# Probabilities times values in the window attention: whole fp32 in two column halves, in place of three fp32r passes

## Chip, cores and metric

One core of a Trainium2 chip runs the whole program. The metric is the device time of one execution in microseconds (us), as the median of several.

## What is computed

Two layers of a decoder trunk over 1024 tokens with 16 learned meta tokens ahead of them. The change lies in the second layer's attention: 16 query heads, 4 key/value heads, head size 64, a window of 128 in blocks of 128 queries, the meta tokens always visible, and one learned sink per head:

```python
def swa_mixer(h, wq, wk, wv, q_norm_w, k_norm_w, sinks, wo):
    q = rms_norm((h @ wq).reshape(b, l, kv, grp, d), q_norm_w) * (d ** -0.5)
    k = rms_norm((h @ wk).reshape(b, l, kv, d), k_norm_w)
    v = (h @ wv).reshape(b, l, kv, d)
    ...
    s_meta = jnp.einsum('bnikgd,bjkd->bnkgij', qb, km)
    s_band = jnp.einsum('bnikgd,bnjkd->bnkgij', qb, kband)      # this block's keys and the block's before
    valid = (rel >= 0) & (rel < SWA_WINDOW) & (n * SWA_BLOCK - SWA_BLOCK + j >= 0)
    s_band = jnp.where(valid[None, :, None, None], s_band, -jnp.inf)
    p = sink_softmax(jnp.concatenate([s_meta, s_band], -1), sink[None, None, :, :, None, None])
    orr = (jnp.einsum('bnkgim,bmkd->bnikgd', p[..., :N_META], vm)
           + jnp.einsum('bnkgij,bnjkd->bnikgd', p[..., N_META:], vband))
    return jnp.concatenate([om, orr], 1) @ wo
```

All inputs and outputs are float32.

## The kernel before

The program is: the first layer's mixer, its FFN, the attention (`swa`), and the second layer's FFN. Activations are kept transposed, features on the 128 partitions and tokens along the free dimension.

Matmuls against weights are done in three passes. An operand is split into a high part, rounded to fp32r, and a low part, the rest, also fp32r (`load_w`, `split`); `gemm` (L147) then adds high x high, high x low and low x high in PSUM. A matmul whose operands are plain F32 is done in whole fp32: the scores (`scp`, L1082), the sums of squares for the head norms (`qkp`, L981), the transposes and the meta part of the output (L1151). The trace shows each of these as two passes.

The attention works on two groups G of eight query heads. A group has two key/value heads s, one on partitions 0 to 63 and the other on 64 to 127, and four tiles t with one query head of each. `attend(G, hook)` goes through the eight query blocks n, and one pair (G, n) is called a block here, sixteen in all:

- `scores(G, n, pmq)`: per t two score matmuls, one per head s, each on its own 64 rows of the array, into two PSUM banks; ACT copies 144 columns out (L1088), VectorE puts the second half in under a mask (L1089), so that one 128-column window holds old keys above the diagonal and new keys below. Then the softmax: maximum and its follow-ups on VectorE (L1094 to L1097), exponentials on ACT (L1100), sum and reciprocal on VectorE (L1101, L1102), scaling on GpSimd (L1103), meta columns copied to `pmq` (L1104).
- `turn(pr)`: transposes a head's four probability tiles into one PSUM bank `ptp` and makes two operands: `all`, the whole 128 x 512, and `own`, the part under the mask U that belongs to this block's keys. Each has a high and a low part: ACT casts the high part (L1113), VectorE subtracts (L1114), and the mask is applied to the high part by VectorE and to the low part by GpSimd (both L1116).
- `out_block(G, n, pmq, pts)`: the weights are values. With v the values of this block and v' those of the block before, the output is v' x all + (v - v') x own. `vparts` splits v and d = v - v' into parts, ACT the high (L1124), GpSimd the low (L1125), each written into a zeroed 192-column tile `vx` whose middle 64 columns stay zero; a slice of 128 columns of it has the values of one head and zeros for the other. So both heads' passes fill all 128 output rows of the bank `po` and add up there. `mm3` makes the three passes (line L1028 in the profile); four matmuls with `vm` add the meta part (L1151), and VectorE copies `po` out (L1153). With n = 0 there is only the `own` term.

Between these pieces a planner puts work that does not depend on them: during `attend(0, ...)` the projections and head norms of group 1, during `attend(1, ...)` the output projections (`outputs`, L147 with `wo`). The planner runs a model of the engines when the program is built, and the queue of every engine is fixed by it.

PSUM in this stage has two banks for `mm`, two for the ring `a` (`ptp`, `pmp`, `po` and others take turns in it), and two pairs of banks for scores.

Of the kernel before, what the change touches and what calls it, by code (L numbers as in the profile page):

```python
# [7 lines left out]
F32 = mybir.dt.float32  # L8
F32R = mybir.dt.float32r
# [3 lines left out]
ALU = mybir.AluOpType  # L13
# [3 lines left out]
P = 128  # L17
# [65 lines left out]
def trunk(tc, hT0, w_in, w_ab, w_out, w_q, w_k, w_v, w_o, w_up, w_down, vec, cst, out):  # L83
    nc = tc.nc
    pe, ve, ac, gp, sp = nc.tensor, nc.vector, nc.scalar, nc.gpsimd, nc.sync
    ctx = ExitStack()
    with ctx:
# [29 lines left out]
        def col(i):  # L117
            return vt[:, i:i + 1]
# [7 lines left out]
        def aux(name, tag="b"):  # L126
            return banks["in"].tile([P, 512], F32, tag=tag, name=name, bufs=banks[tag])
# [817 lines left out]
        def swa(h, sqp):  # L945
# [5 lines left out]
            with tc.tile_pool(name="l1", bufs=1, reuse_waits="tile") as lp:  # L951
# [4 lines left out]
                ve.tensor_scalar(qn, col(V_QN), -0.125 / 128, None, ALU.mult)  # L956
                kn = lp.tile([P, 1], F32, name="kn")
                ve.tensor_scalar(kn, col(V_KN), -1.0 / 128, None, ALU.mult)
                zero = lp.tile([P, 1], F32, name="zero")
                ve.memset(zero, 0.0)  # L960
                qg = [[None] * 4, [None] * 4]
                kx = [None, None]
                vraw = [None, None]
                vm = [None, None]
                vx = []
                for i in range(4):
                    a = lp.tile([P, 192], F32R, name=f"vxh{i}")
                    b = lp.tile([P, 192], F32R, name=f"vxl{i}")
                    ve.tensor_copy(a, zero.broadcast_to([P, 192]))
                    ve.tensor_copy(b, zero.broadcast_to([P, 192]))  # L970
                    vx.append((a, b))

                def head_norms(d, wcol, ring=None, cs=CH):

                    for c0, n in cs:
                        x = d[:, c0:c0 + n]
                        sq = sqp.tile([P, 348], F32, tag="sq", name="sq", bufs=2)[:, :n]
                        y, z = (lp.tile([P, 348], F32, tag=nm, name=nm, bufs=2)[:, :n] for nm in ("hy", "hz"))
                        ac.activation(sq, x, AF.Square)
                        p2 = aux("qkp", ring) if ring else mmp("qkp")  # L980
                        pe.matmul(p2[:, :n], ct[:, C_BD:C_BD + P], sq, start=True, stop=True)  # L981
                        with tc.issue_after(lnexp):
                            ac.activation(y, p2[:, :n], AF.Ln, scale=1.0 / 64, bias=epsc)
                        ac.activation(y, y, AF.Exp, scale=-0.5)
                        ac.activation(z, y, AF.Square)

                        ve.scalar_tensor_tensor(z, p2[:, :n], 64 * EPS, z, ALU.add, ALU.mult)
                        ve.scalar_tensor_tensor(y, z, -192.0, y, ALU.add, ALU.mult)
                        ve.scalar_tensor_tensor(x, x, wcol, y, ALU.mult, ALU.mult)
# [16 lines left out]
                def values(G, vr):  # L1006
# [14 lines left out]
                    vm[G] = lp.tile([P, 4, P], F32, name=f"vm{G}")  # L1021
                    for t in range(4):
                        ve.tensor_scalar(vm[G][:, t, :], v4, ct[:, C_T4 + t:C_T4 + t + 1], None, ALU.mult)

                def mm3(ps, w, x, start, stop):
                    (wh, wl), (xh, xl) = w, x
                    for j, (a, b) in enumerate(((wh, xh), (wh, xl), (wl, xh))):
                        pe.matmul(ps, a, b, start=(start and j == 0), stop=(stop and j == 2))  # L1028

                def meta_queries(G):  # L1030
                    sc = lp.tile([NM, 8, NM], F32, tag="msc", name="msc")
# [31 lines left out]
                U = ct[:, C_U:C_U + P]  # L1063
# [43 lines left out]
                def turn(pr):  # L1107

                    tp = aux("ptp", "a")
                    for t in range(4):  # L1110
                        pe.transpose(tp[:, t * P:(t + 1) * P], pr[:, t, :], ident)
                    x, y = (lp.tile([P, 2, 512], F32R, tag="hl", name=nm, bufs=4) for nm in ("all", "own"))
                    ac.copy(x[:, 0, :], tp)  # L1113
                    ve.tensor_tensor(x[:, 1, :], tp, x[:, 0, :].bitcast(F32), ALU.subtract)  # L1114
                    for j, eng in enumerate((ve, gp)):
                        eng.tensor_tensor(y[:, j].rearrange("p (t i) -> p t i", t=4),  # L1116
                                          x[:, j].bitcast(F32).rearrange("p (t i) -> p t i", t=4),
                                          U.unsqueeze(1).broadcast_to([P, 4, P]), ALU.mult)
                    return x, y

                def vparts(pair, src):
                    d3 = lambda a: a.rearrange("p (a i) -> p a i", a=3)[:, 0::2, :]
                    src = src.rearrange("p (a i) -> p a i", a=2)
                    ac.copy(d3(pair[0]), src)  # L1124
                    gp.tensor_tensor(d3(pair[1]), src, d3(pair[0].bitcast(F32)), ALU.subtract)  # L1125

                def out_block(G, n, pmq, pts):

                    tok = slice(NM + n * P, NM + (n + 1) * P)
                    tp = aux("pmp", "a")  # L1130
                    pe.transpose(tp[:, :P], pmq.rearrange("p t s m -> p (t s m)"), ident)
                    pmt = lp.tile([P, P], F32, tag="pmt", name="pmt", bufs=2)
                    ac.copy(pmt, tp[:, :P])
                    v = vraw[G][:, n, :]
                    if n < 7:
                        vparts(vx[n % 2], v)
                    if n:
                        d = lp.tile([P, P], F32, tag="vd", name="vd", bufs=2)
                        gp.tensor_tensor(d, v, vraw[G][:, n - 1, :], ALU.subtract)
                        vparts(vx[2 + n % 2], d)  # L1140
                        use = [(0, vx[(n - 1) % 2]), (1, vx[2 + n % 2])]
                    else:
                        use = [(1, vx[0])]
                    po = aux("po", "a")
                    for s in range(2):
                        vs = slice(64 * s, 64 * s + P)
                        for j, w in use:
                            x = pts[s][j]
                            mm3(po, [a[:, vs] for a in w], (x[:, 0], x[:, 1]), s == 0 and j == use[0][0], s == 1 and j == 1)
                        for t in range(4 if s == 0 else 0):  # L1150
                            pe.matmul(po[:, t * P:(t + 1) * P], vm[G][:, t, :], pmt, start=False, stop=False)  # L1151
                    for t in range(4):
                        ve.tensor_copy(qg[G][t][:, tok], po[:, t * P:(t + 1) * P])  # L1153

                def attend(G, hook):
                    def first(n):
                        pmq = lp.tile([P, 4, 2, NM], F32, tag="pmq", name="pmq", bufs=2)
                        return pmq, scores(G, n, pmq)

                    nxt = first(0)  # L1160
                    for n in range(8):
                        pmq, prs = nxt
                        if n < 7:
                            nxt = first(n + 1)
                        out_block(G, n, pmq, [turn(pr) for pr in prs])
                        if n == 0:
                            meta_queries(G)
                        hook(n)
# [75 lines left out]
        with ExitStack() as st:  # L1244

            psum(st, "ps1", 2, 2, 0)
            h = swa(h, st.enter_context(tc.tile_pool(name="sqp", bufs=1, reuse_waits="tile")))
# [71 lines left out]
```

## Time and profile before

| | |
|---|---|
| time, median of 3 runs | 2404.53 us (2403.84 to 2405.23) |
| the profiled execution | 2401.72 us, span 2399.9 us |
| mean granted TensorE clock | 0.994 |
| busy: PE, DVE, ACT, POOL | 2336.4, 1655.3, 982.3, 477.0 us |
| first and last score matmul begin | 1370.5 and 1630.3 us |
| first and last pass of probabilities x values begin | 1395.6 and 1657.8 us |

PE is TensorE's matmuls, PEld its weight loads, DVE is VectorE, ACT ScalarE, POOL GpSimd. Times within the span are counted from its start. The profile names instructions by their line, with "out<-in" by the tiles' names. The duration of a single matmul in it holds its way through the array too, and the next one starts before it ends; the rate of a stream is read from the chain of waits, which gives a group's length from start to start.

### The profile page before, as it was taken

What the parts mean: (1) busy time and instruction counts of PE and PEld (TensorE: products, weight loads), DVE (VectorE), ACT (ScalarE), POOL (GpSimd) and SP (SyncE); (2) the same over time, 40 slices, a digit from 0 to 9 for tenths busy, and PEclk for the clock granted to TensorE, in tenths of its full rate; (3) what the DMA queues carried; (4) which work ended last, traced back from release to release, by engine and by line L of the source; (5) the groups of instructions that cost most, each with busy time, mean ns of one, the idle gap of its engine ahead of it and who ended that gap; (6) DMA issues with size and microseconds to landing.
All of it is one profiled execution on the core that took longest, in us unless ns stands there. A gap on an engine that the chain in (4) does not pass through costs nothing.

```text
span 2399.9 us, 40060 instructions
## 1 busy us (share of the span) xinstructions
PE 2336.4 (97%) x16060; PEld 2205.4 (92%) x16060; DVE 1655.3 (69%) x2840; ACT 982.3 (41%) x1980; POOL 477.0 (20%) x417
## 2 busy tenths in 40 slices
PE   8999999999999999999999999999799999999999
PEld 7999999999999999999999987878799999988887
DVE  8886735667877777776536578778977777778432
ACT  6545213434444444432225456656644444433110
POOL 1123323430000000022225245454000000002221
PEclk9999999999999999999999999999999999999999
DMA  4234434141222222253213100202222222235222
GB/s 138 84 122 138 160 118 142 54 174 74 80 72 80 80 80 80 74 195 118 86 61 107 45 27 19 88 27 76 103 90 81 78 79 79 80 142 166 82 66 101
DMA packets 93481, 224.83 MB, mean 94 GB/s; under 512 B 18672, under 2 KB 30264, under 8 KB 93296
## 3 DMA queue, kind: packets, MB, share of 16 engines
q1 hardware_dynamic: 93296, 222.28, 27.3%
q8 instruction: 126, 2.06, 0.4%
q14 instruction: 59, 0.48, 0.1%
HBM read 166.08 MB, written 56.15 MB: 93 GB/s over the span
## 4 chain that ended last, share of the span: by engine, by line
PE 82%; DVE 11%; ACT 3%; DMA 2%; issue 1%; POOL 0%; SPq 0%; ACTq 0%; DVEq 0%; POOLq 0%
PE mm L147 38%; PE A L825 20%; PE C L825 15%; PE po L1028 1%; DVE qt L251 1%; PE scp L1082 1%; ACT sc L1100 1%; DVE yl L171 1%; PE qkp L981 1%; DVE Xd L499 0%; DVE X L752 0%; DVE fq L497 0%; ACT xh L182 0%; PE po L1151 0%; DVE all L1114 0%
## 5 line engine op out<-in xcount | busy, mean ns | idle before, releaser
L825 PE MATMUL A<-X,whi 128*128 128x260 f32 (+1 forms) x2816 | 511.7, 283 | 6.6 <-ACT whi L814 2.5
L147 PE MATMUL mm<-y,wdh 128*128 128x346 f32 (+2 forms) x1760 | 471.1, 350 | 1.6 <-DVE r L903 1.6
L825 PEld LDWEIGHTS A<-X,whi 128*128 128x128 f32 x2816 | 432.6, 189 | 8.0 <-ACT whi L814 2.7
L825 PE MATMUL C<-X,whi 128*128 128x260 f32 (+1 forms) x2112 | 393.2, 284 | 8.1 <-DVE v L894 5.9
L825 PE MATMUL A<-X,wlo 128*128 128x260 f32 (+1 forms) x1408 | 391.9, 282 | 0.6 <-DVE wlo L815 0.6
L135 POOL TENSOR_TENSOR wdl<-wdr,wdh 128x512 fp32r<-128x512 f32 (+1 forms) x80 | 120.1, 1502 | 1310.0 <-ACT wdh L134 1305.5
L147 PEld LDWEIGHTS mm<-y,wdh 128*128 128x128 f32 x1760 | 315.1, 188 | 32.7 <-DVE r L903 2.0
L825 PEld LDWEIGHTS C<-X,whi 128*128 128x128 f32 x2112 | 330.4, 190 | 9.3 <-DVE v L894 6.3
L147 PE MATMUL mm<-y,wdl 128*128 128x346 f32 (+2 forms) x880 | 307.7, 350 | 0.0
L825 PE MATMUL C<-X,wlo 128*128 128x260 f32 (+1 forms) x1056 | 297.3, 284 | 0.0
L825 PEld LDWEIGHTS A<-X,wlo 128*128 128x128 f32 x1408 | 263.4, 189 | 0.8 <-DVE wlo L815 0.8
L939 DVE TENSOR_TENSOR h<-mm,h 128x346 f32<-128x346 f32 (+2 forms) x200 | 115.5, 584 | 201.8 <-PE mm L147 201.2
L825 PEld LDWEIGHTS C<-X,wlo 128*128 128x128 f32 x1056 | 200.2, 190 | 0.0
L147 PEld LDWEIGHTS mm<-y,wdl 128*128 128x128 f32 x880 | 165.5, 188 | 16.1 <-POOL wdl L135 0.7
L815 DVE TENSOR_TENSOR wlo<-sa,whi 128x1024 fp32r<-128x1024 f32 x44 | 53.9, 1225 | 161.4 <-ACT whi L814 161.4
L134 ACT CAST wdh<-wdr 128x512 fp32r<-128x512 f32 (+1 forms) x80 | 53.1, 663 | 254.8 <-PE mm L147 215.3
L814 ACT CAST whi<-sb 128x512 fp32r<-128x512 f32 x88 | 54.6, 621 | 133.7 <-PE C L825 131.1
L147 PE MATMUL mm<-xl,wqkvh 128*128 128x346 f32 (+1 forms) x288 | 95.3, 331 | 1.5 <-DVE xl L183 1.5
L147 PE MATMUL mm<-xh,wqkvh 128*128 128x346 f32 (+1 forms) x288 | 95.7, 335 | 0.7 <-DVE row L269 0.7
L814 ACT CAST whi<-sa 128x1024 fp32r<-128x1024 f32 x44 | 46.1, 1048 | 115.2 <-PE A L825 115.1
L147 PE MATMUL mm<-xh,wqkvl 128*128 128x346 f32 (+1 forms) x288 | 92.4, 322 | 0.0
L928 ACT CAST y<-yf 128x346 fp32r<-128x346 f32 (+2 forms) x110 | 54.6, 536 | 91.8 <-DVE yf L927 70.9
(402 smaller groups left out, 5235.3 us busy)
## 6 DMA issues: line engine op xcount, KB each, us to landing
wg<-in_w_up SPq DMA_DIRECT2D x44, 512.0 KB, 3.3
wv<-in_w_up SPq DMA_DIRECT2D x44, 512.0 KB, 3.5
wdr<-in_w_down SPq DMA_DIRECT2D x48, 256.0 KB, 2.6
fy<-sg SPq DMA_DIRECT2D x22, 520.0 KB, 2.7
yf<-fy SPq DMA_DIRECT2D x22, 520.0 KB, 4.5
fy<-sg SPq DMA_DIRECT2D x22, 516.0 KB, 2.7
yf<-fy SPq DMA_DIRECT2D x22, 516.0 KB, 3.8
wdr<-in_w_down SPq DMA_DIRECT2D x32, 320.0 KB, 3.4
```

The costliest lines, as they stand in the source:

```text
L134: ac.copy(hi, raw)
L135: eng.tensor_tensor(lo, raw, hi.bitcast(F32), ALU.subtract)
L147: pe.matmul(ps[:, :n], a[:, j, :], b[:, c0:c0 + n], start=(i == 0), stop=(i == last))
L171: ve.tensor_tensor(dst_l, src, dst_h.bitcast(F32), ALU.subtract)
L251: ve.scalar_tensor_tensor(d, buf[:, pad + c0 - i:pad + c0 - i + n], taps[W - 1 - i], tmp[:, :n], ALU.mult, ALU.add)
L814: ac.copy(hi, src)
L815: ve.tensor_tensor(lo, src, hi.bitcast(F32), ALU.subtract)
L825: pe.matmul(ps[:, b, :q], a[:, at + k, :], x[:, c], start=(start and n == 0), stop=(n == 11), skip_group_check=not start)
L928: ac.copy(yh[:, s], yf[:, s])
L939: ve.tensor_tensor(hn[m][:, s], ps[:, :n], hn[m][:, s], ALU.add)
L981: pe.matmul(p2[:, :n], ct[:, C_BD:C_BD + P], sq, start=True, stop=True)
L1028: pe.matmul(ps, a, b, start=(start and j == 0), stop=(stop and j == 2))
```

## The change

`turn` no longer splits. ACT copies the transposed probabilities to `all` in F32, VectorE multiplies the same PSUM bank with U into `own` in F32. GpSimd's mask is gone. `vparts`, `mm3`, the four `vx` pairs and their eight zeroing casts are gone; the values are used as they stand in `vraw`, and d stays on GpSimd. In `out_block` each head's matmul takes 64 columns of values as weights and writes 64 output rows: head 0 into rows 0 to 63 of `po` and head 1 into rows 64 to 127, so the two stand in different column halves of the array. There are four such matmuls in a block (two with n = 0), in whole fp32. The meta matmuls come after them instead of between the heads. The ring `hl` has eight buffers of half the size.

```diff
-                vx = []
-                for i in range(4):
-                    a = lp.tile([P, 192], F32R, name=f"vxh{i}")
-                    b = lp.tile([P, 192], F32R, name=f"vxl{i}")
-                    ve.tensor_copy(a, zero.broadcast_to([P, 192]))
-                    ve.tensor_copy(b, zero.broadcast_to([P, 192]))
...
-                    x, y = (lp.tile([P, 2, 512], F32R, tag="hl", name=nm, bufs=4) for nm in ("all", "own"))
-                    ac.copy(x[:, 0, :], tp)
-                    ve.tensor_tensor(x[:, 1, :], tp, x[:, 0, :].bitcast(F32), ALU.subtract)
-                    for j, eng in enumerate((ve, gp)):
-                        eng.tensor_tensor(y[:, j]..., x[:, j]..., U..., ALU.mult)
+                    x, y = (lp.tile([P, 512], F32, tag="hl", name=nm, bufs=8) for nm in ("all", "own"))
+                    four = lambda a: a.rearrange("p (t i) -> p t i", t=4)
+                    ac.copy(x, tp)
+                    ve.tensor_tensor(four(y), four(tp), U.unsqueeze(1).broadcast_to([P, 4, P]), ALU.mult)
...
-                    if n < 7:
-                        vparts(vx[n % 2], v)
                     if n:
                         d = lp.tile([P, P], F32, tag="vd", name="vd", bufs=2)
                         gp.tensor_tensor(d, v, vraw[G][:, n - 1, :], ALU.subtract)
-                        vparts(vx[2 + n % 2], d)
-                        use = [(0, vx[(n - 1) % 2]), (1, vx[2 + n % 2])]
+                        use = [(0, vraw[G][:, n - 1, :]), (1, d)]
...
-                    for s in range(2):
-                        vs = slice(64 * s, 64 * s + P)
-                        for j, w in use:
-                            x = pts[s][j]
-                            mm3(po, [a[:, vs] for a in w], (x[:, 0], x[:, 1]), s == 0 and j == use[0][0], s == 1 and j == 1)
-                        for t in range(4 if s == 0 else 0):
-                            pe.matmul(po[:, t * P:(t + 1) * P], vm[G][:, t, :], pmt, start=False, stop=False)
+                    for j, w in use:
+                        for s in range(2):
+                            vs = slice(64 * s, 64 * s + 64)
+                            pe.matmul(po[vs, :], w[:, vs], pts[s][j], start=(j == use[0][0]), stop=False,
+                                      skip_group_check=True)
+                    for t in range(4):
+                        pe.matmul(po[:, t * P:(t + 1) * P], vm[G][:, t, :], pmt, start=False, stop=True,
+                                  skip_group_check=True)
```

How the queues change is shown at three places. In the rows, `vxh` and `vxl` are high and low parts of values (one number for v', another for d), `vraw` the values, `vd` is d. A row of a matmul stands for one instruction of the program, "x2" for two alike; the last numbers are partitions x free size of the result. Line numbers before and after differ.

TensorE's queue at block n = 1 of group 0, before:

```order
L1028 MATMUL po<-all,vxh_13622 128x512 x2
L1028 MATMUL po<-all,vxl_13623 128x512
L1028 MATMUL po<-own,vxh_13634 128x512 x2
L1028 MATMUL po<-own,vxl_13635 128x512
L1151 MATMUL po<-pmt,vm_14354 128x128 x4
```

and after, the same block and the one behind it:

```order
L1122 MATMUL po<-all,vraw_14317 64x512 x2
L1122 MATMUL po<-own,vd 64x512 x2
L1125 MATMUL po<-pmt,vm_14336 128x128 x4
L971 MATMUL qkp<-sq,ct 128x346
L1096 MATMUL ptp<-ct,sc 128x128 x4
```

The four rows ahead of L1151 stood a second time behind it for the other head; two rows of two whole-fp32 matmuls have taken the place of all eight. In the next block the two heads of the `own` pair are parted: one L1122 row with `vd` stands alone, then come two scores, a transpose, twelve projection matmuls, and then the other.

VectorE's queue in group 1, in the blocks that have no output projections between them, before:

```order
L1094 TENSOR_REDUCE sc<-sc 128x4
L1114 TENSOR_TENSOR all<-ptp,all 128x512
L1116 TENSOR_TENSOR own<-all,ct 128x512
L1089 COPY_PREDICATED sc<-ct,scp 128x128
L1095 TENSOR_TENSOR sc<-sc,vt 128x4
```

and after:

```order
L1079 TENSOR_REDUCE sc<-sc 128x4
L1100 TENSOR_TENSOR own<-ptp,ct 128x512
L1074 COPY_PREDICATED sc<-ct,scp 128x128
L1080 TENSOR_TENSOR sc<-sc,vt 128x4
L1074 COPY_PREDICATED sc<-ct,scp 128x128
```

The subtraction has left the queue, and the mask reads PSUM.

GpSimd's queue in the same blocks, before:

```order
L1116 TENSOR_TENSOR own<-all,ct 128x512 x2
L1103 TENSOR_TENSOR sc<-sc 128x576
L1104 COPY pmq<-sc 128x4x16
L1125 TENSOR_TENSOR vxl_13627<-vraw_14959,vxh_13626 128x2x64
L1103 TENSOR_TENSOR sc<-sc 128x576
L1125 TENSOR_TENSOR vxl_13631<-vd,vxh_13630 128x2x64
L1104 COPY pmq<-sc 128x4x16
```

and after:

```order
L1088 TENSOR_TENSOR sc<-sc 128x576
L1089 COPY pmq<-sc 128x4x16
L1088 TENSOR_TENSOR sc<-sc 128x576
L1089 COPY pmq<-sc 128x4x16
L1114 TENSOR_TENSOR vd<-vraw_14915 128x128
```

The masks and the low parts of the values have left it; scaling, the meta columns and the difference stay.

More of the change, by code (lines that the diff above doesn't have):

```diff
@@ L958, in swa @@
                 ve.tensor_scalar(kn, col(V_KN), -1.0 / 128, None, ALU.mult)
-                zero = lp.tile([P, 1], F32, name="zero")
-                ve.memset(zero, 0.0)
                 qg = [[None] * 4, [None] * 4]
@@ L964, in swa @@
                 vm = [None, None]
-                vx = []
-                for i in range(4):
-                    a = lp.tile([P, 192], F32R, name=f"vxh{i}")
-                    b = lp.tile([P, 192], F32R, name=f"vxl{i}")
-                    ve.tensor_copy(a, zero.broadcast_to([P, 192]))
-                    ve.tensor_copy(b, zero.broadcast_to([P, 192]))
-                    vx.append((a, b))
                 def head_norms(d, wcol, ring=None, cs=CH):
@@ L1023, in values @@
                         ve.tensor_scalar(vm[G][:, t, :], v4, ct[:, C_T4 + t:C_T4 + t + 1], None, ALU.mult)
[L1025 to L1028, printed above, removed]
                 def meta_queries(G):
@@ L1111, in turn @@
                         pe.transpose(tp[:, t * P:(t + 1) * P], pr[:, t, :], ident)
-                    x, y = (lp.tile([P, 2, 512], F32R, tag="hl", name=nm, bufs=4) for nm in ("all", "own"))
-                    ac.copy(x[:, 0, :], tp)
-                    ve.tensor_tensor(x[:, 1, :], tp, x[:, 0, :].bitcast(F32), ALU.subtract)
-                    for j, eng in enumerate((ve, gp)):
-                        eng.tensor_tensor(y[:, j].rearrange("p (t i) -> p t i", t=4),
-                                          x[:, j].bitcast(F32).rearrange("p (t i) -> p t i", t=4),
-                                          U.unsqueeze(1).broadcast_to([P, 4, P]), ALU.mult)
-                    return x, y
[L1121 to L1125, printed above, removed]
+                    x, y = (lp.tile([P, 512], F32, tag="hl", name=nm, bufs=8) for nm in ("all", "own"))
+                    four = lambda a: a.rearrange("p (t i) -> p t i", t=4)
+                    ac.copy(x, tp)
+                    ve.tensor_tensor(four(y), four(tp), U.unsqueeze(1).broadcast_to([P, 4, P]), ALU.mult)
+                    return x, y
                 def out_block(G, n, pmq, pts):
@@ L1139, in out_block @@
                         gp.tensor_tensor(d, v, vraw[G][:, n - 1, :], ALU.subtract)
-                        vparts(vx[2 + n % 2], d)
-                        use = [(0, vx[(n - 1) % 2]), (1, vx[2 + n % 2])]
+                        use = [(0, vraw[G][:, n - 1, :]), (1, d)]
                     else:
-                        use = [(1, vx[0])]
+                        use = [(1, v)]
                     po = aux("po", "a")
-                    for s in range(2):
-                        vs = slice(64 * s, 64 * s + P)
-                        for j, w in use:
-                            x = pts[s][j]
-                            mm3(po, [a[:, vs] for a in w], (x[:, 0], x[:, 1]), s == 0 and j == use[0][0], s == 1 and j == 1)
-                        for t in range(4 if s == 0 else 0):
-                            pe.matmul(po[:, t * P:(t + 1) * P], vm[G][:, t, :], pmt, start=False, stop=False)
+                    for j, w in use:
[6 more added lines that the diff above has]
+                                  skip_group_check=True)
                     for t in range(4):
```

## The prediction

> **What bounds the kernel now.** I read the engines' shares first, then the stretches of the stage that the change touches, then the chain of waits inside them. By the shares TensorE is the bound:
>
> ```profile
> span 2399.9 us, 40060 instructions
> PE 2336.4 (97%) x16060; PEld 2205.4 (92%) x16060; DVE 1655.3 (69%) x2840; ACT 982.3 (41%) x1980; POOL 477.0 (20%) x417
> ```
>
> A share of the whole program says nothing of one stage, so I cut the attention (from 1370 to 1660 us) where its chain of waits changes engine. Columns: length, then busy time and count of PE, its weight loads, DVE, ACT and POOL, then the granted clock.
>
> ```profile
> 1370.00:1426.00 56.00, 56.00 (x365) 48.60 (x364) 39.27 (x115) 30.35 (x114) 28.31 (x32) 1.00 0.09 31
> 1426.00:1494.00 68.00, 64.08 (x367) 48.78 (x366) 55.85 (x147) 44.81 (x162) 38.97 (x45) 1.00 0.07 23
> 1494.00:1594.00 100.00, 98.11 (x593) 83.60 (x591) 73.33 (x212) 53.06 (x193) 43.84 (x51) 0.98 0.18 64
> 1594.00:1637.00 43.00, 35.46 (x199) 25.69 (x198) 36.60 (x104) 27.22 (x110) 26.93 (x31) 0.96 0.04 13
> 1637.00:1660.00 23.00, 23.00 (x143) 21.84 (x144) 16.43 (x39) 11.57 (x32) 13.12 (x10) 1.00 0.18 59
> ```
>
> PE is full, or nearly so, in the first, third and last stretch: there a microsecond of PE work is a microsecond of time. In the second it idles 3.9 us and in the fourth 7.5 us, while VectorE is busy for 82% and 85%. The chain of waits in the fourth (start, length, what) shows who holds PE up:
>
> ```profile
> 1611.78 0.60 DVE all L1114
> 1612.38 0.60 DVE own L1116
> ...
> 1613.19 0.95 DVE sc L1095
> ...
> 1614.35 0.59 DVE all L1114
> 1614.94 0.60 DVE own L1116
> 1615.54 0.66 DVE sc L1094
> 1616.20 0.51 DVE sc L1096
> ...
> 1616.74 0.51 ACT sc L1100 x2
> ...
> 1617.34 1.19 ACT sc L1100 x6
> ```
>
> So there are two prices: PE work counts in the full stretches, VectorE's chain in the other two.
>
> **PE work, before.** A block is one step n of attend for one group; there are sixteen. The chain at a block in a full stretch, and the counts of po's passes with their durations in ns (least, median, most):
>
> ```profile
> 1421.29 1.12 PE scp L1082 x8
> 1422.41 1.56 PE po L1028 x6
> 1423.97 0.89 PE po L1151 x8
> 1424.86 1.39 PE po L1028 x6
> 1426.24 0.59 PE qkp L981 x2
> ```
>
> ```profile
> L1151 PE MATMUL po<-pmt,vm x128: 270/275/402, 1396.3 to 1656.5; 128*128 128x128 f32 x128
> L1028 PE MATMUL po<-own,vxh x64: 387/396/967, 1395.6 to 1657.5; 128*128 128x512 f32 x64
> L1028 PEld LDWEIGHTS po<-own,vxh x64: 186/188/333, 1395.5 to 1657.3; 128*128 128x128 f32 x64
> ```
>
> Six passes take 1.39 us, 0.232 us each (the 1.56 includes leaving the score matmuls). A block has twelve, 2.78 us; a block with n = 0 has only the "own" half, six, 1.39 us. The four matmuls with vm are whole fp32 and stand as eight passes: a whole-fp32 matmul is two passes.
>
> **PE work, after.** A block has four whole-fp32 matmuls with 64 columns of weights and 512 moving columns, so eight passes. The price of such a pass comes from two other whole-fp32 lines:
>
> ```profile
> L621 PE MATMUL onp<-fq,ct x16: 590/592/697, 378.5 to 461.0; 128*128 128x512 f32 x16
> L981 PE MATMUL qkp<-sq,ct x60: 442/453/762, 1304.8 to 1528.1; 128*128 128x346 f32 x40, 128*128 128x334 f32 x16, 128*128 128x348 f32 x4
> ```
>
> Their medians differ by 139 ns over 166 columns: 0.84 ns per column, 0.43 us for 512 (the two qkp passes above, 346 columns, take 0.59 us, 0.85 per column). So a pass is 1.85 times as dear as before, and the change pays on PE only if the two heads run at the same time. The trace has no two matmuls in different column halves. It has its nearest kin in L1082, where the heads stand in different row halves: eight passes of 272 columns at 0.84 would be 1.83 us one after the other, and the row says 1.12: four times 0.228 = 0.91, plus 0.21 for getting into and out of the split array. Row halves thus run fully side by side. I take the same for column halves: four slots of 0.43 plus 0.21 = 1.93 us, against 2.78. The other end is eight slots, 3.65 us. With n = 0 it is 1.07 or 1.93 us, against 1.39. Fourteen blocks save 0.85 and two save 0.32: 12.5 us; in one block the order puts twelve projection matmuls between the two heads' "own" matmuls, which costs two lone passes, 0.86. PE: **-11.7 us** side by side, and one after the other 14 x 0.87 + 2 x 0.54 = **+13.3 us**. I take the first, by the row of L1082.
>
> The Trainium skill's page "TensorE: Matmul & The Clock Gate" (Part 3) says that column tiles run concurrently much as row tiles do and gives 2.38 times for three of them; by it the PE term is the first one, and no run so far shows it for whole fp32. The same section says that a weight load overlaps a running matmul only if their row groups differ, which two column halves never do; that is the last rival below.
>
> **VectorE and GpSimd.** The change takes out the subtraction L1114, GpSimd's half of L1116 and both lines of vparts, and leaves L1116 on VectorE, reading PSUM.
>
> ```profile
> L1114 DVE TENSOR_TENSOR all<-ptp,all x32: 660/681/692, 1389.2 to 1650.0; 128x512 fp32r<-128x512 f32 x32
> L1116 DVE TENSOR_TENSOR own<-all,ct x32: 673/681/1581, 1389.8 to 1650.6; 128x512 fp32r<-128x512 f32 x32
> L1116 POOL TENSOR_TENSOR own<-all,ct x32: 1642/1666/1758, 1390.8 to 1650.7; 128x512 fp32r<-128x512 f32 x32
> L1095 DVE TENSOR_TENSOR sc<-sc,vt x32: 141/156/2208, 1379.5 to 1642.6; 128x4 f32<-128x4 f32 x32
> ```
>
> The surviving mask op is priced at 0.68 us whichever memory it reads, since L1114 (PSUM) and L1116 (SBUF) have one median. Removed from VectorE: 32 x 0.68 = 21.8 us. There is more: L1095 works on four columns, and its median is 156 ns, yet some take 2208. Here is why (VectorE, then GpSimd, same moments; start, length):
>
> ```profile
> 1613.09 1.05 DVE L1095 TENSOR_TENSOR sc<-sc,vt 128x4 f32<-128x4 f32 x1
> 1616.12 0.58 DVE L1096 TENSOR_SCALAR sc<-sc 128x4 f32<-128x4 f32 x1
> 1616.89 0.15 DVE L1095 TENSOR_TENSOR sc<-sc,vt 128x4 f32<-128x4 f32 x1
> ```
>
> ```profile
> 1612.46 1.67 POOL L1116 TENSOR_TENSOR own<-all,ct 128x512 fp32r<-128x512 f32 x1 [0.61 <-DVE all L1114]
> 1615.02 1.66 POOL L1116 TENSOR_TENSOR own<-all,ct 128x512 fp32r<-128x512 f32 x1 [0.90 <-DVE all L1114]
> ```
>
> The long L1095 and the long L1096 end when GpSimd's op ends (1614.13 and 1616.68). GpSimd's mask thus holds up small VectorE ops, about 0.9 and 0.4 us a block here, and it goes away. The skill's page "SBUF — State Buffer" (section Who interferes with whom) calls this an exclusive port pair shared by VectorE and GpSimd; these rows agree, and the sum would be the same without it.
>
> Other removed work is priced at nothing: vparts' casts on ACT and subtractions on GpSimd lie beside PE in the full stretches, and in the others their share of the chain is inside the terms below. The copy of ptp by ACT stays. The deeper ring for all/own has as many bytes as before. The surviving mask waits for ACT's copy of the same ptp, as L1114 did. The eight casts at the start of swa hold VectorE from 1292.15 to 1296.53, but PE has projections to do meanwhile and loses only one wait of 0.8 us behind them:
>
> ```profile
> 1292.15 0.31 DVE vxh L969
> 1292.46 2.41 DVE vxl L970
> ...
> 1296.36 0.17 DVE vxl L970
> ```
>
> ```profile
> L147 PE MATMUL mm<-xh,wqh 128*128 128x346 f32 x128 | 42.0, 328 | 0.8 <-DVE kr L995 0.8
> ```
>
> I take -0.5 of it.
>
> **The sum, stretch by stretch.** Blocks are counted by L1151's eight passes each; the row of the fourth stretch gives three:
>
> ```profile
> L1151 PE MATMUL po<-pmt,vm x24: 270/275/402, 1606.1 to 1626.9; 128*128 128x128 f32 x24
> ```
>
> First: blocks n = 0 and 1, -0.32 - 0.85 = -1.2. Second: four blocks counted likewise, each with two L1114 (1.2 us) and stalls like those shown (up to 1.3 us) on or near the chain, 10 us at most; PE allows 4 x 0.85 - 0.86 + 3.9 idle = 6.4; half of the first, 5, lies below that, and I take -5. Third: five blocks counted likewise, one with n = 0, -3.7; of its 1.9 us idle about half, -1.0; a granted clock of 0.98 over 100 us is 2 us lost to a slow clock after a pause of PE, -1.3. Together -6. Fourth: three blocks, each with two L1114 (1.2 us) and about 1.3 us of stall on the chain, so -7.5, and part of the slow clock; PE would allow 3 x 0.85 + 7.5 + 1.7 = 11.8; I take -8. Fifth: two blocks, -1.7. With the start, **-22.4 us**. What follows (output projection, norm, FFN) keeps its order on all engines and moves up as a whole. The profiled execution took 2401.72 us (span 2399.9), 2.8 under the median of 2404.53 shown; against that median the sum gives **2382**.
>
> **Rivals.**
> Relief without effect (0.14): VectorE's chain gets shorter, but ACT takes its place. For it: ACT's exponentials follow L1096 on the same chain. Against: ACT is busy 27 of 43 us in the fourth stretch, VectorE 37. Then only the PE term and little else counts, -12: 2392.
> Half overlap (0.09): the two passes of one matmul run in order, so the second head starts one pass late: five slots instead of four, 0.43 us more in each of sixteen blocks, 6.9 us: 2389. Against: L1082's eight passes fit four slots.
> No overlap in columns (0.12): +13.3 on PE. But the stretches with idle PE absorb their part. First +1.4, second -0.4 (3.5 more work less 3.9 idle), third +4.0 less 1.9 idle less 1.2 clock, fourth 2.6 less 7.5 idle, fifth +1.7, start -0.5: -1.8, about 2403, no change. For it: the two moving streams together read twice what L1082's do, which use half the partitions each.
> The other side (0.07): no overlap, and each pass also waits for its own weight load. A load's place is a block's eight passes; its price lies between 0 and the 0.19 us of a full load (0.188 in the row of weight loads above), say 0.1: 0.8 us a block, +12 on the last case, 2415. It decides once the exposed part of a load exceeds about 0.05 us. Against: in the full-array streams of this trace loads are hidden, six in 1.39 us.
> The forecast itself has 0.58, from -16 to -29 us: 2375 to 2388.
>
> **How the numbers follow.** What this kernel's measurement can tell from no change is about 0.2%, 4.8 us. Faster: 0.58 + 0.14 + 0.09 + 0.02 of the no-overlap case = 0.83; same 0.07 and slower 0.03 of that case; slower with the last rival 0.10. The range runs from the lower end of the forecast, a little widened, 2373, to the middle of the no-overlap case, 2403; outside lie the last rival, half of the one before, and a few hundredths below.
>
> **What would show it.** In the trace after: the passes into po start in pairs a few ns apart, and a block's eight take near 1.9 us on PE (near 3.6 refutes the PE term). L1095's longest falls well below 2208 ns and its mean to about 0.3 us. PE's idle time in the fourth stretch falls from 7.5 to under 4 us. VectorE's mask from PSUM stays at 0.68 us. If the blocks take 1.9 us and the time is still above 2392, the term of the second and fourth stretch was wrong.

## The result, and the profile after

The changed kernel takes **2385.93 us** (median of 4 runs, 2384.45 to 2391.28) against 2404.88 us (2403.84 to 2406.29) for the kernel before on the same chip: a ratio of 0.9922, 95% interval 0.991 to 0.9934. That is 19.0 us less, where 22.4 was forecast. The profiled execution took 2385.68 us.

The page of the kernel after, its span and the engines' shares:

```profile
span 2383.9 us, 39785 instructions
PE 2324.3 (98%) x16000; PEld 2182.5 (92%) x16000; DVE 1615.8 (68%) x2799; ACT 973.4 (41%) x1952; POOL 408.2 (17%) x357
```

PE has lost 12 us of busy time, VectorE 40, GpSimd 69, and PE's idle time fell from 63.5 us (2399.9 - 2336.4) to 59.6.

The stretches of the attention after, cut where its chain of waits changes engine (columns as before: length, busy time and count of PE, its weight loads, VectorE, ACT and GpSimd, granted clock, DMA):

```profile
1374.00:1429.00 55.00, 55.00 (x359) 46.30 (x360) 33.59 (x113) 28.58 (x109) 19.77 (x22) 1.00 0.10 33
1429.00:1491.00 62.00, 57.87 (x339) 40.87 (x337) 41.34 (x134) 39.81 (x146) 18.78 (x25) 1.00 0.06 23
1491.00:1588.00 97.00, 96.19 (x595) 77.67 (x595) 65.73 (x211) 52.83 (x195) 26.08 (x36) 0.98 0.18 66
1588.00:1622.00 34.00, 29.70 (x179) 19.07 (x178) 28.14 (x98) 24.95 (x102) 12.20 (x16) 1.00 0.04 16
1622.00:1643.00 21.00, 21.00 (x133) 17.77 (x133) 12.51 (x32) 11.25 (x32) 7.44 (x6) 1.00 0.25 85
```

The five stretches were 56, 68, 100, 43 and 23 us long, 290 together; now they are 269. The fourth is the one that shrank most for its length: PE idles 4.3 us there, not 7.5, and its clock is full. (The sign that was set for it, under 4 us, is narrowly missed.) The second idles as much as before (4.1 against 3.9 us).

The chain of waits at the same block as was shown of before:

```profile
1424.40 1.12 PE scp L1067 x8
1425.52 1.87 PE po L1122 x8
1427.38 1.09 PE po L1125 x8
1428.47 0.60 PE qkp L971 x2
```

From the end of the scores to `qkp` it is 2.96 us, where it was 1.56 + 0.89 + 1.39 = 3.84. Eight whole-fp32 passes take 1.87 us: the two heads run side by side. In the trace the passes of such a pair begin 6 to 7 ns apart, as the prediction asked. The eight passes with `vm` take 1.09 instead of 0.89 us: the 0.20 is the price of leaving the split array, and it shows up in the line behind.

One line's instructions each: the passes into `po`, VectorE's mask, and the two small VectorE operations that GpSimd used to hold up (ns: least, median, most):

```profile
L1122 PEld LDWEIGHTS po<-all,vraw x56: 132/134/137, 1425.4 to 1636.8; 128*64 128x64 f32 x56
L1122 PE MATMUL po<-own,vd x56: 592/592/643, 1426.4 to 1638.1; 128*64 128x512 f32 x56
...
L1100 DVE TENSOR_TENSOR own<-ptp,ct x32: 678/686/693, 1392.5 to 1633.7; 128x512 f32<-128x512 f32 x32
...
L1080 DVE TENSOR_TENSOR sc<-sc,vt x32: 143/156/1551, 1382.8 to 1623.6; 128x4 f32<-128x4 f32 x32
...
L1081 DVE TENSOR_SCALAR sc<-sc x32: 146/162/2250, 1383.5 to 1623.7; 128x4 f32<-128x4 f32 x32
```

The mask from PSUM costs 0.686 us, the 0.68 that was assumed. L1080's longest (it was L1095, 2208 ns) is 1551; L1081's longest is 2250 (it was L1096, 2131). The relief of the small operations is partial.

**Four microseconds that have nothing to do with the change.** At the attention's first projection the profiled execution of after is 3.9 us behind that of before, although both ran the same instructions up to there. The rows of the timeline, before and then after:

```profile
1292.13 0.40 PE L147 MATMUL mm<-xh,wkh 128*128 128x348 f32 x1 [0.54 <-DVE zero L960]
```

```profile
1296.06 0.40 PE L147 MATMUL mm<-xh,wkh 128*128 128x348 f32 x1 [0.54 <-DVE kn L958]
```

It begins at 173 us, in the first layer. PE's waits there (us in total, times, longest), before and then after:

```profile
PE kq L471 <- DVE qk L307: 0.8, 1, 0.8
```

```profile
PE kq L471 <- DVE qk L307: 3.1, 1, 3.1
```

PE waits 2.3 us longer for VectorE's `qk`. The DMA ahead of `qk` landed after 4.68 us instead of 3.73, and `qk` itself took 2.71 us instead of 1.24: it began at 173.22 us, behind an operation of GpSimd (172.40 to 174.83 us). In before it began first (172.07 against 172.23 us), and there GpSimd's operation is the long one, 3.32 us instead of 2.43. After this pause the granted clock is at half for 3.4 us, which costs another 1.7. Most later profiles show this pause, the second profile of after among them. The three that don't (before, `vector_sub_back` and `q_copies_shared`) stand 2.8, 2.5 and 7.6 us under the medians of their kernels, so the pause is one reason why a profile and its median differ. So medians are compared below, and inside a profile the attention alone.

### The profile page after: what moved, and what is told of

Its sections match the earlier page's. It is cut to its first block, busy times and chain, and to the rows that moved or that the text cites. A ratio compares the mean times of both kernels' runs of the same rounds, so it can differ in the third digit from the quotient of the medians.

```text
span 2383.9 us, 39785 instructions
## 1 busy us (share of the span) xinstructions
PE 2324.3 (98%) x16000; PEld 2182.5 (92%) x16000; DVE 1615.8 (68%) x2799; ACT 973.4 (41%) x1952; POOL 408.2 (17%) x357
## 4 chain that ended last, share of the span: by engine, by line
PE 84%; DVE 10%; ACT 3%; DMA 1%; issue 1%; POOL 0%; SPq 0%; ACTq 0%; DVEq 0%; POOLq 0%
PE mm L147 40%; PE A L825 20%; PE C L825 15%; PE scp L1067 1%; DVE qt L251 1%; PE po L1122 1%; DVE X L752 1%; PE qkp L971 1%; PE po L1125 1%; ACT xh L182 0%; DVE Xd L499 0%; DVE yl L171 0%; DVE fq L497 0%; DMA rb<-rq 0%; PE ptp L1096 0%
```

## The experiments

Two theories stood at the start. **Sum**: the gain is PE's shorter work plus VectorE's and GpSimd's relief, each about half, and they add. **PE alone** or **relief alone**: one of them carries it, and the other is hidden. Each ratio below is to the kernel before on the same chip, with its 95% interval; after itself was run once more for comparison.

> The changed kernel once more, beside the runs it is compared with here: ratio to before 0.992, and a profile to see whether the pause of about 4 us that the profile of after has at 173 us, in the first layer and ahead of anything the change touches, comes again. If it belongs to the program, it is there; if to the single execution, it may be missing as in the profile of before.

It came out at 2387.78 us, 0.992 (0.9909 to 0.9932).

**Without the column halves.** Whole fp32, but each matmul with 128 columns of weights, the other head's 64 being zeros; VectorE's and GpSimd's work as after.

```diff
...
-gp.tensor_tensor(d, v, vraw[G][:, n - 1, :], ALU.subtract)
+gp.tensor_tensor(cols(d), cols(v), cols(vraw[G][:, n - 1, :]), ALU.subtract)    # 192 columns, the middle 64 zero
...
-vs = slice(64 * s, 64 * s + 64)
-pe.matmul(po[vs, :], w[:, vs], pts[s][j], start=(j == use[0][0]), stop=False,
+pe.matmul(po, w[:, 64 * s:64 * s + P], pts[s][j], start=(j == use[0][0] and s == 0), stop=False,
...
```

> Whole fp32 as in the changed kernel, but each head's values stand in 128 weight columns with zeros for the other head, so both heads write all 128 rows of po and nothing stands side by side. Vector work as in the changed kernel (values are stored padded once per group; the difference is written padded by GpSimd). Theory, PE work and vector relief both count: eight passes of 0.43 us follow each other, about 3.45 us a block (after: 1.87); PE's extra 13 us over before is nearly eaten by its former idle time, about 2403 us. Rival 1, only PE's work counts: 2405 + 13 = 2418. Rival 2, only the vector relief counts: about 2388.

2401.1 us, 0.9974 (0.9963 to 0.9985). The chain at the same block:

```profile
1426.44 1.12 PE scp L1074 x8
1427.56 3.63 PE po L1128 x8
1431.19 0.89 PE po L1131 x8
```

Eight passes one after the other take 3.63 us, and the meta passes are back at 0.89. Side by side saves 4.52 - 2.96 = 1.56 us a block; the kernel loses 0.0054 of its time, 13 us, by giving that up. It still beats before, by relief alone.

**Relief alone.** Three fp32r passes on the full array as in before, with VectorE, GpSimd and ACT working as after. The low parts are left out: all three passes multiply the rounded operands.

```diff
...
-pe.matmul(po[vs, :], w[:, vs], pts[s][j], start=(j == use[0][0]), stop=False,
-          skip_group_check=True)
+for i in range(3):
+    pe.matmul(po, w[:, 64 * s:64 * s + P], pts[s][j],
+              start=(j == use[0][0] and s == 0 and i == 0), stop=False, skip_group_check=True)
```

> PE's work as before (three fp32r passes over 128 zero-padded columns, twelve a block), vector work as in the changed kernel. It leaves out the low parts: all three passes multiply the rounded high parts. Theory: no gain on PE, but the stretches where VectorE's chain held PE up shrink, about 2395 us, with PE's idle time in the fourth stretch well under 7.5 us. Rival 1, only PE's work counts: 2405. Rival 2, only the relief counts: 2386 to 2388.

2393.78 us, 0.9944 (0.9932 to 0.9957): relief alone is worth 13.5 us, and the step from there to after is 0.0024, 6 us (the two intervals together allow 2 to 10). The stage of this run by its window, to be set beside after's, which stands with the subtraction below (269.00 us, PE busy 259.77):

```profile
1374.00:1649.00 275.00, 269.22 (x1655) 226.66 (x1655) 179.89 (x583) 156.73 (x582) 84.06 (x105) 1.00 0.12 41
```

PE idles 5.8 us here and 9.2 in after. So a part of what the column halves take off PE comes back as waiting.

**PE's gain alone.** After, with VectorE's subtraction and GpSimd's mask put back as operations whose output nobody reads.

```diff
 ac.copy(x, tp)
+ve.tensor_tensor(lp.tile([P, 512], F32, tag="spare2", name="spare2", bufs=2), tp, x, ALU.subtract)
 ve.tensor_tensor(four(y), four(tp), U.unsqueeze(1).broadcast_to([P, 4, P]), ALU.mult)
+gp.tensor_tensor(four(lp.tile([P, 512], F32, tag="spare", name="spare", bufs=2)), four(x), ...)
```

> The changed kernel plus the vector work it had dropped, as work nobody reads: per transposed head a 128x512 subtraction from PSUM on VectorE (0.68 us) ahead of the mask and a 128x512 mask on GpSimd (1.67 us) after the copy. Column halves stay. Theory: the PE gain of about 10 stays, the relief goes, about 2395 us, and the small VectorE ops are long again (mean of the maximum with the sink back from about 0.2 to 0.5 us). Rival 1, only PE's work counts: 2386. Rival 2, only the relief counts: 2405.

2406.43 us, 0.9993 (0.9984 to 1.0002). Missed: the column halves by themselves bring nothing that can be measured, 1.7 us with an interval from -0.5 to 3.8. That is less than the 6 us that they bring behind the relief, but the intervals of the two overlap, so it is not shown that the parts fail to add. In the stage (1375 to 1666 us here, 1370 to 1660 before) PE is busy 274.43 of 291 us instead of 276.64 of 290, so it idles 16.6 us instead of 13.4. The next two runs put the operations back one at a time.

> The changed kernel plus a 128x512 mask per head on GpSimd that nobody reads; VectorE's queue stays as in the changed kernel. With both dropped pieces back the gain was gone (2406 against 2386), so they cost 20 us together. Theory: most of it is GpSimd, in two ways, the small VectorE ops that its reads hold up and its own queue, in which the scaling of the probabilities waits behind the mask and the transposes wait for the scaling: 12 us or more over the changed kernel, 2398 or above. Rival: VectorE's own time is what counts, and this run stays within 5 us of the changed kernel.

GpSimd's mask alone: 2394.09 us, 0.9942 (0.993 to 0.9954), 6 us slower than after, half of what was expected.

> The changed kernel plus a 128x512 subtraction per head on VectorE that nobody reads (0.68 us, 21.8 us in all); GpSimd stays relieved. Theory: VectorE has room now (busy 67% in the second stretch), so most of it is hidden: 2 to 6 us over the changed kernel. Rival, VectorE's time is what counts: 12 us or more over it.

VectorE's subtraction alone: 2404.27 us, 0.9985 (0.9975 to 0.9995), 16.5 us slower than after, for 32 operations of 0.68 us = 21.8 us. The rival that VectorE's chain is the price held; I had taken GpSimd's hold-ups for the larger part, and it is the other way round. Where the time went, by the stage's windows, after and then with the subtraction:

```profile
1374.00:1643.00 269.00, 259.77 (x1598) 201.69 (x1599) 181.29 (x582) 157.43 (x582) 84.27 (x105) 0.99 0.13 45
```

```profile
1374.00:1661.00 287.00, 272.12 (x1602) 204.78 (x1601) 201.00 (x615) 157.25 (x578) 84.26 (x105) 0.98 0.12 43
```

Of 18 us more, PE idles 5.7 (14.9 against 9.2), and PE itself is busy 12.4 longer with the same matmuls. The groups of PE's matmuls in these windows (busy, mean ns, idle before) show part of it, after first:

```profile
L1067 PE MATMUL scp<-kx,q 64*128 64x272 f32 (+1 forms) x256 | 42.2, 423 | 2.3 <-DVE sc L1074 2.2
...
L1096 PE MATMUL ptp<-ct,sc 128*128 128x128 f32 x128 | 20.1, 279 | 4.0 <-POOL sc L1088 4.0
...
L1122 PE MATMUL po<-own,vd 128*64 128x512 f32 x56 | 15.5, 593 | 0.0
```

```profile
L1067 PE MATMUL scp<-kx,q 64*128 64x272 f32 (+1 forms) x256 | 46.7, 436 | 0.8 <-DVE sc L1074 0.8
...
L1096 PE MATMUL ptp<-ct,sc 128*128 128x128 f32 x128 | 20.6, 288 | 8.0 <-POOL sc L1088 7.9
...
L1123 PE MATMUL po<-own,vd 128*64 128x512 f32 x56 | 18.8, 602 | 0.0
```

The transposes wait twice as long for the end of the softmax (GpSimd's scaling L1088, which stands behind VectorE's sum and reciprocal). The `own` passes take 3.3 us more, the `all` passes 0.9 and the scores 4.5. One cause is the order: the planner knows of the longer chain and sets PE's queue otherwise. In the built queues of after, one of the sixteen pairs of `own` matmuls has other work between its two heads; with the subtraction there are four, and the scores stand in 55 groups instead of 51. A parted pair runs alone in its half of the array and costs 0.99 us more (2.86 against 1.87, shown with `mask_on_gpsimd` below), so three of them make 3.0. The other cause is the slow clock, 10.2 us of the stage against 3.4, of which half the difference, 3.4 us, is lost. The scores in the two stretches at half clock, with the subtraction:

```profile
1611.95:1615.36 3.41, 2.12 (x8) 1.19 (x8) 0.79 (x3) 0.43 (x2) 0.50 0.00 0
1622.19:1629.01 6.82, 2.56 (x8) 1.01 (x8) 1.85 (x7) 1.67 (x7) 0.50 0.01 2
```

They make 4.68 us of PE; in after's one stretch (1490.63 to 1494.04 us) the scores take 1.53. Half of the difference, 1.6 us, is the clock's part of the scores' 4.5. The same view for `po` gives 2.13 us against none, so 1.1 is its part there, and with the 3.0 for the parted pairs the 4.2 us of `po` are accounted for. What is left of the 12.4 is 2.9 us in the scores and about 3 in other lines; no run says why.

**Does the order of the two heads matter?** The loops over heads and operands exchanged, so that a head's `all` and `own` stand together.

```diff
-for j, w in use:
-    for s in range(2):
+for s in range(2):
+    for j, w in use:
```

> The changed kernel with the four matmuls of a block in the other order: both of head 0 (all, own), then both of head 1. Theory: TensorE starts matmuls in the order of its queue and pairs only neighbours in different halves, so only one boundary overlaps: five to eight slots, 2.2 to 3.5 us a block in place of 1.87, 2390 to 2400 us. Rival: each column half runs through its own matmuls whatever stands between, 1.87 us a block and 2386 us.

2386.66 us, 0.9918 (0.9905 to 0.9931), no different from after. The chain has the same block:

```profile
1426.30 1.87 PE po L1122 x8
```

Eight passes again fit four slots, although the queue names four passes of the first head and then four of the second. The rows of PE give the order in which they began:

```profile
1426.23 1.08 PE L1122 MATMUL po<-all,vraw 128*64 128x512 f32 x4
1427.14 1.03 PE L1122 MATMUL po<-own,vd 128*64 128x512 f32 x4
```

In the queue the second head's two `all` passes stand behind the first head's two `own` passes; here all four `all` passes begin first. A half of the array takes its next matmul without waiting for an earlier one in the other half. The Trainium skill's page "TensorE: Matmul & The Clock Gate" (Part 3, The mechanism) calls matmuls "strict FIFO, no reordering" in start and end; by that the first head's four passes, which share their columns, would have held the second head's back, for seven slots or 3.0 us. This run doesn't agree. (That two passes of one head can't share a slot is shown further down, where a lone matmul's two passes take 1.00 us.) In this run's queue four `own` pairs are parted, against one in after, and no loss is seen: three parted pairs, about 3 us, are as much as the intervals.

**GpSimd's weight work.** The low parts of `wo` and of group 1's `wq` moved to VectorE, since one of them held L1081 for 2.2 us in the second stretch. VectorE's, then GpSimd's operations at that place in after:

```profile
1482.53 2.25 DVE L1081 TENSOR_SCALAR sc<-sc 128x4 f32<-128x4 f32 x1
```

```profile
1482.39 2.36 POOL L135 TENSOR_TENSOR wol<-wor,woh 128x1024 fp32r<-128x1024 f32 x1 [7.16 <-ACT woh L134]
```

The edit is one argument in each of the two calls:

```diff
-qg[G][t] = project(load_w(w_q[G * 4 + t], KT, "wq"), f"q{G}{t}", QCH)
+qg[G][t] = project(load_w(w_q[G * 4 + t], KT, "wq", ve if G else gp), f"q{G}{t}", QCH)
...
-w = load_w(w_o[i, G], 8, "wo", eng)
+w = load_w(w_o[i, G], 8, "wo", ve)
```

> The changed kernel with the low parts of the twelve weight tiles loaded during the attention (four of wq, eight of wo) made by VectorE, 1.23 us each, in place of GpSimd, 2.4 us each. In the profile of after one such GpSimd op holds a four-column VectorE op for 2.1 us. Theory: if GpSimd's ops are what holds the chain, the removal of these is worth more than the 15 us of added VectorE work, which lie beside PE: 0 to 5 us faster than the changed kernel. Rival: VectorE's added work lands on its chain, and it is slower by up to 8.

2390.32 us, 0.9926 (0.9914 to 0.9938): no gain. The hold-up is gone, L1081's longest is 326 ns. What took its place isn't shown: VectorE is busy 188.12 us of the stage instead of 181.29, three `own` pairs are parted instead of one, and behind 1482 us the chain of this run goes through ACT's casts and exponentials.

**Is it VectorE's busy time?** That was the theory left: 21.8 us of VectorE cost 16.5. If so, taking work off VectorE should pay. Three versions do.

```diff
-ve.tensor_tensor(four(y), four(tp), U.unsqueeze(1).broadcast_to([P, 4, P]), ALU.mult)
+gp.tensor_tensor(four(y), four(x), U.unsqueeze(1).broadcast_to([P, 4, P]), ALU.mult)    # mask_on_gpsimd
+(gp, ve)[s].tensor_tensor(four(y), four((x, tp)[s]), ...)                                # mask_split
...
-ve.tensor_copy(qg[G][t][:, tok], po[:, t * P:(t + 1) * P])
+(ve.tensor_copy if t < 2 else ac.copy)(qg[G][t][:, tok], po[:, t * P:(t + 1) * P])       # q_copies_shared
```

> The changed kernel with both mask multiplications of a block moved from VectorE (0.69 us each, from PSUM) to GpSimd, which reads ACT's copy in SBUF; nothing is left out. VectorE loses 32 x 0.69 = 21.9 us; GpSimd's multiplication took 1.32 us in the run with both additions. Theory (VectorE's time per head is what the stage pays for, as the run with the subtraction put back showed with 0.5 us of time for each us of VectorE): VectorE's relief is worth up to 10 us, GpSimd's mask costs about 6, so 2382 to 2388 and a ratio near 0.991. Rival (the own half now comes 0.6 to 1.3 us later, behind ACT's copy and, for the second head, behind the first head's mask, and PE waits for it before a block): 5 to 15 us slower than the changed kernel, ratio 0.994 to 0.998.

2405.7 us, 1.0002 (0.9993 to 1.0011). The whole gain is gone, more than the rival gave, though VectorE is busy for less than in after (stage by its window: 172.86 of 285 us against 181.29 of 269). (The theory's 0.5 us for each us of VectorE was a slip: 16.5 for 21.8 is 0.76.)

```profile
1376.00:1661.00 285.00, 275.52 (x1605) 203.75 (x1602) 172.86 (x548) 157.39 (x579) 126.05 (x137) 1.00 0.12 42
```

PE idles 9.5 us, no more than in after, and the clock is full; PE is busy 15.8 us longer. One group holds nearly all of that, 29.2 us where after has 15.5:

```profile
L1122 PE MATMUL po<-own,vd 128*64 128x512 f32 x56 | 29.2, 606 | 0.0
```

The chain shows how:

```profile
1428.32 1.86 PE po L1122 x6
1430.18 0.66 PE scp L1067 x4
1430.84 0.59 PE ptp L1096 x4
1431.43 1.00 PE po L1122 x2
1432.43 1.09 PE po L1125 x8
```

GpSimd's mask in this run, by its line:

```profile
L1100 POOL TENSOR_TENSOR own<-all,ct x32: 1264/1285/1747, 1395.9 to 1653.5; 128x512 f32<-128x512 f32 x32
```

So the second head's `own` comes 1.3 us after the first's. The planner puts scores and transposes into the gap, so the two `own` matmuls are apart: two slots for the `all` pair, two for a lone `own` and two more later, 2.86 us for eight passes, in place of 1.87. In the built queue 15 of the 16 `own` pairs are parted. This measures the side by side running in place: lost for half of the passes, it costs 15 us of PE, and the kernel 20.

> The changed kernel with the first head's mask on GpSimd (from ACT's copy in SBUF) and the second head's left on VectorE (from PSUM); nothing is left out. VectorE loses 16 x 0.69 = 11 us, the two masks of a block can run beside each other. Theory (VectorE's time per head is what the stage pays for): half of 11 us gained, half of the 6 us for GpSimd's masks lost, about 2 us faster than the changed kernel, ratio 0.991. Rival (GpSimd's longer operation holds up VectorE's small ones and comes late): 2 to 8 us slower, ratio 0.993 to 0.996.

2391.44 us, 0.9939 (0.9925 to 0.9952): 0.0019 more than after, 4 to 5 us. Three pairs are parted.

> The changed kernel with two of the four copies of po into q of each block moved from VectorE to ACT; nothing is left out. VectorE loses 32 x 0.28 = 9 us of the stage, ACT gains about as much. Theory (VectorE is the engine that the chain of a head goes through, ACT has slack): the two halves run beside each other and VectorE is freed, 2 to 5 us faster than the changed kernel, ratio 0.990 to 0.991. Rival (the copies come at a block's end, where nothing but the end of the stage waits for them, and ACT's exponentials, which are on the chain, get later): no change to 5 us slower, ratio 0.992 to 0.994.

2388.56 us, 0.9923 (0.991 to 0.9936): no change, with 32 copies of 0.28 us, 9 us, off VectorE and no pair parted. So VectorE's busy time as such isn't the price: it depends on where the work stands. What the subtraction made longer is the way from `ptp` to the operands and to the next softmax, and with it PE's order; that this is the price is argued from the waits and queues above, not shown by a run of its own. None of the versions beats after.

## Why the prediction held, and where its working was off

**PE term, -11.7 us: right as work, too large as time.** Four slots and an overhead for the split array, 1.93 us, were taken from the score matmuls; measured are 1.87 us and 0.20 in the next line. Behind scores a block saves 3.84 - 2.96 = 0.88 us; elsewhere, where before had no 0.17 for leaving the scores (1.56 against 1.39), 3.67 - 2.96 = 0.71. Fourteen blocks: 10 to 12 us. The 3.65 us without overlap fit the 3.63 that were measured, though the 0.21 in them were meant for a split array that `full_fp32` doesn't have; what stands there is the 0.17 for leaving the scores. In time the PE term brought about half, 6 us behind the relief (`full_3pass_relief` against after) and nothing measurable without it: the prediction priced a microsecond of PE work in a full stretch at one, and PE waits more in after (9.2 us of the stage) than with the relief alone (5.8). The rule that weight loads overlap a running matmul only in another row group (the Trainium skill, "TensorE: Matmul & The Clock Gate", Part 3, The mechanism) did not bite: the halves share all rows, each load takes 0.134 us, the first two loads for `own` begin at 1425.93 us together with passes of `all`, and eight passes are 0.15 us longer than four slots of 0.43.

**The stages.** The first and last copies of `po` into q, before and then after:

```profile
L1153 DVE COPY q<-po x64: 260/281/292, 1399.0 to 1658.8; 128x128 f32<-128x128 f32 x64
```

```profile
L1128 DVE COPY q<-po x64: 260/281/293, 1401.1 to 1641.9; 128x128 f32<-128x128 f32 x64
```

The last is 16.9 us earlier, after an entry that was 3.9 later: from its first projection on the attention is 20.8 us shorter, forecast 22.4. The first scores (1370.5 us before, 1373.9 after) are 3.4 us later, so 0.5 is gained ahead of them, as was forecast for the casts. Followed through the sixteen blocks' copies in the two timelines in the same way, the gain from the entry on is 1.7 us at the second block (forecast 1.7), 10.9 at the eleventh (12.7), 19.4 at the fourteenth (20.7) and 20.8 at the end (22.4). The fourth stretch alone gives 8.4, forecast 8. The term that was mis-sized is that of the second stretch, -5: at the sixth block, which ends it, 3.1 us are gained in all, where 6.7 were forecast; about 5 more come with the seventh, and second and third together give 9.3 of 11. In it the chain turned to other work: the head norms of group 1 (`hy`, `hz`, L973 to L978), exponentials, and the one L1081 held for 2.2 us.

**What was late next in the fourth stretch.** The chain of after there:

```profile
1590.33 0.65 DVE sc L1079
1590.98 0.42 DVE h L1188
1591.41 0.60 DVE own L1100
1592.01 0.21 DVE sc L1074
1592.21 1.45 DVE sc L1080
...
1598.14 1.20 ACT sc L1085 x6
```

It is still VectorE, one operation behind the other, with one hold-up left (L1080, 1.45 us), and ACT's exponentials after that. The rival "relief without effect" (2392) gave ACT the whole place; ACT has a part of it.

**Relief: right in sum, wrong in its division.** The prediction added PE's gain and the relief stretch by stretch and gave the stalls under GpSimd's operations about the weight of the subtraction (1.3 and 1.2 us a block). L1080 and L1081 (L1095 and L1096 before) did get shorter. Their groups in the attention's window (busy us, mean ns), before and then after:

```profile
L1095 DVE TENSOR_TENSOR sc<-sc,vt 128x4 f32<-128x4 f32 x32 | 16.5, 514 | 0.0
L1096 DVE TENSOR_SCALAR sc<-sc 128x4 f32<-128x4 f32 x32 | 11.9, 372 | 0.3
```

```profile
L1081 DVE TENSOR_SCALAR sc<-sc 128x4 f32<-128x4 f32 x32 | 7.6, 238 | 0.3
L1080 DVE TENSOR_TENSOR sc<-sc,vt 128x4 f32<-128x4 f32 x32 | 6.6, 207 | 0.0
```

But put back by itself, the mask on GpSimd costs 6 us and the subtraction 16.5. Of the 22.4 us forecast, 11.7 were PE's and 10.7 the relief's; the runs give the relief 13.5 by itself and PE about 6 behind it. The sum came near because one share was priced too high and the other too low, and that much of it is luck. An order of PE's queue that parts the heads takes PE's gain away again, as `mask_on_gpsimd` shows with 15 pairs; in after one pair of sixteen is parted, which was counted (0.86 us; the lone two passes take 1.00 here). With both operations back, four pairs are parted, too few to explain the lost gain; the rest there is PE's idle time (3.2 us more than before) and a clock of 0.98 instead of 0.99, and is not separated further.

On the hold-ups, the Trainium skill's page "SBUF — State Buffer" (Who interferes with whom) has it that a VectorE instruction with at most one input in SBUF, outside its two-port modes, doesn't contend with GpSimd. The rows agree as far as they go: the mask, which reads `ptp` from PSUM, took 693 ns at most, though 8 of the 32 overlap one of GpSimd's operations, while L1080, with both inputs in SBUF, went up to 1551. L1081 has one input in SBUF and was held too, up to 2250; no run shows whether it is in a two-port mode, so it settles nothing.

**Left open.** Of the 18 us that the subtraction costs in its profile (16.5 by the medians), 12.1 are accounted for: PE's idle 5.7, the slow clock 3.4, parted pairs 3.0. The scores' other 2.9 us and the rest are not. A version with the subtraction and the order of after was not run, so what the order alone costs there is not measured. Whether PE's gain and the relief add is not settled by the intervals.

## What to carry to other kernels

Two matmuls that use half of the array's columns each run at the price of one here, also in whole fp32 (1.87 us for eight passes against 3.63), but not where other work stands between them in the queue (2.86 us): a second operand that comes one operation later can part them, because the planner fills the gap. So look where the operands of such a pair come from, and read from the chain whether their passes stand as one group. And when a change relieves two engines, put each relief back alone before crediting it: here one cost 6 us and the other 16.5. Work saved on an engine that is nearly full isn't time saved either, until its idle time after the change is read: of the 10 to 12 us less work on PE, about 6 became time.

## What the hardware showed that was not expected

- The halves of the array's columns take their matmuls independently of the order in the queue: 1.87 us for eight passes in both orders (`head_by_head`).
- Leaving the split array costs 0.20 us in the work that follows (1.09 against 0.89 us for the same eight passes), entering about 0.15 (1.87 less four slots of 0.43 behind the scores, 1.00 less two slots behind transposes).
- A load of 64 columns of fp32 weights takes 0.134 us, where one of 128 took 0.188.
- The mask of 128 x 512 takes 1.285 us on GpSimd from plain fp32, against 1.666 in before's form with an fp32r result, and 0.686 on VectorE.
- A whole-fp32 transpose stands as one pass, not as two as was said ahead: the 128 transposes of the attention are the 128 `ptp` passes in the rows above.
